# Gate and up of a feed-forward block by half-size products with features on partitions, and the residual stream parked in DRAM

## The chip, the core and the metric

The kernel runs on one core of one Trainium2 chip. The metric is the device time of one execution in microseconds; lower is better. Engines are named as the profile names them: PE (TensorE, with PEld for its weight loads), DVE (VectorE), ACT (ScalarE), POOL (GpSimd) and SP (SyncE, which issues nearly all DMAs).

## The reference

A trunk of two layers, each a SwiGLU half-step, a gated token mixing (stick-breaking, forgetting and memory attention) and a second SwiGLU half-step, with RMSNorm before and after each. There are 512 tokens of width 1024, all in float32. The change touches the four SwiGLU blocks only (D_FF = 2816 = 22 tiles of 128 features):

```python
def _swiglu(t, w_gate, w_up, w_down):
    return (jax.nn.silu(t @ w_gate) * (t @ w_up)) @ w_down

def reference(x, mem, ...):
    ...
    for l in range(DEPTH):
        f = _swiglu(_rmsnorm(h, ffn1_pre_g[l]), ffn1_w_gate[l], ffn1_w_up[l], ffn1_w_down[l])
        h = h + 0.5 * _rmsnorm(f, ffn1_post_g[l])
        u = _rmsnorm(h, mix_pre_g[l])
        ...
        h = h + _rmsnorm(merged @ w_out[l], mix_post_g[l])
        f = _swiglu(_rmsnorm(h, ffn2_pre_g[l]), ffn2_w_gate[l], ffn2_w_up[l], ffn2_w_down[l])
        h = h + 0.5 * _rmsnorm(f, ffn2_post_g[l])
    return h
```

## The kernel before

**Arithmetic.** Every float32 operand is split into a high part h (rounded for TensorE) and a low part l = x - h. A product is then three matmuls into one PSUM bank: h·h, h·l and l·h (`mm3`, L204; `split`, L177, makes the parts with a cast on ACT, L180, and a subtraction on DVE, L181). Weights come from DRAM in units of 512 KB (`Unit`): a load into a ring of two raw buffers, then a split into one of four `wh` and one of four `wl` buffers of 128 x 1024 elements. A weight buffer can be written again when the matmuls on the unit four earlier have read it.

**Order.** `Queue` holds the jobs of TensorE in the order in which they run; when a job starts, the units of the next jobs are split, four of them ahead (AHEAD, `load_ahead`), and loads are issued as far ahead as raw buffers are free (`fetch_ahead`). Between blocks, chains for the normalisation are woven in by estimated times (`weave`). Each engine executes its instructions in the order in which they stand in its queue, which is fixed when the kernel is built. DMAs stand in SP's queue, so a DMA whose buffer isn't free yet holds up those behind it.

**A feed-forward block** (`ffn`; "a0", "c0", "a1", "c1" in the names: tile `ga` is a gate weight of block a0 or a1, `uc` an up weight of c0 or c1). The normalised input stands transposed in `us`: model features on partitions, 512 tokens along the free dimension. Gate and up run by pairs of feature tiles (256 features): a 128x128 block of weights is stationary, 512 tokens move. The first pair runs in two token halves (`halved`), since the input arrives by token tiles; the other ten pairs in full width (`gates`, `ups`). `hidden` evaluates silu on ACT (L616) and the product with up on DVE.

**The down projection** of feature tiles 0 to 15 is already done by half-size products: in two sets ci = 0, 1 of eight tiles, the matrices are cut in 2 x 2 blocks and seven products of blocks take the place of eight (Winograd's form of Strassen's method). Number n = 0 to 6 names a product. The weight side is a `BlockUnit`: it loads a block, for n >= 2 subtracts blocks on DVE (L327, L335, L338), and is split. The other side, `first_factor`, adds and subtracts blocks of the hidden rows `hr` (L684 to L690) and is split as well. Three PSUM bank pairs hold partial sums (`SUM`: products 0, 3, 5 and 6 share one pair, 2 and 4 another); behind a product its sum is copied by ACT (L722) or added by DVE (L724) to the block `TO[n]` of the output. A product stays open in its bank while the next one of the same pair adds to it, so the next may not begin before the sum was read. In the queue one such product follows each gate or up job from pair 6/7 on, so that each is spread over two jobs. Tiles 16 to 21 go through plain matmuls in `down`, which also runs the end of the block with the next normalisation.

**The residual stream** `hT` is four tiles of 512 KB under the tag "o", which has eight buffers (`BUFS`, L102), from one normalisation to the next.

Of the kernel before, what the change touches and what calls it, by code (L numbers as in the profile page):

```python
# [9 lines left out]
F32 = mybir.dt.float32  # L10
# [7 lines left out]
P = 128  # L18
# [4 lines left out]
def kernel(  # L23
# [209 lines left out]
    class Unit:  # L233
# [11 lines left out]
        def ring(self):  # L245

            return self.place == "raw"

        def fetch(self):
            if not self.waits():  # L250
                return
            Q.fetched += self.ring()
# [27 lines left out]
    class BlockUnit(Unit):  # L280
# [15 lines left out]

        def ring(self):
            return self.BLOCKS[self.n] is not None
# [6 lines left out]
        def fetch(self):  # L305
# [3 lines left out]
            if self.n == 2:  # L309
                tc.keep_in_program_order(self.block(self.keep.get(0, self.k0), (0, 1)))  # L310
            if self.n == 3:
                tc.keep_in_program_order(self.block(self.keep.get(1, self.k0), (1, 1)))
            if self.ring():
                Q.fetched += 1
                self.raw = stile([P, self.nk, self.ncol], "raw", "raw_" + self.name, F32)
                self.block(self.raw[:], self.BLOCKS[self.n])

        def load(self):
# [3 lines left out]
            t = self.keep.get(0, self.k0) if self.n >= 2 else None  # L322
            b = self.keep.get(1, self.k0) if self.n >= 3 else None
            if self.n < 2:
                src = self.raw[:]
            elif self.n == 2:
                nc.vector.tensor_tensor(t, t, self.raw[:], ALU.subtract)  # L327
                src = t
            elif self.n == 3:
                nc.vector.tensor_tensor(t, b, t, ALU.subtract)  # L330
                src = t
            elif self.n == 4:
                src = b
            elif self.n == 5:
                nc.vector.tensor_tensor(b, b, self.raw[:], ALU.subtract)  # L335
                src = b
            else:
                nc.vector.tensor_tensor(t, t, self.raw[:], ALU.subtract)  # L338
                src = t
# [1135 lines left out]
```

## Time and profile before

| what | value |
|---|---|
| time, median of 3 runs | 2456.08 us (2452.51 to 2456.12) |
| span of the profiled execution | 2448.5 us |
| granted TensorE clock, mean | 0.999 |
| PE busy | 2432.6 us, 99% |
| DVE busy | 1550.9 us, 63% |
| ACT busy | 1181.7 us, 48% |
| data moved by DMA | 280.5 MB, 115 GB/s on the mean |

The span runs from the first to the last instruction of one profiled execution; the time of a run is measured on the device, without the profiler. A group of instructions is written as line, engine, operation, output<-inputs, shapes and count, then busy time in all and the mean of one in ns, then the idle time of the engine just before them and what ended it. In a timeline the first column is the start and the second the duration in us. Matmuls are pipelined: a matmul of 512 columns shows a duration of 0.39 us, but the next one starts sooner, so the pace is read from starts.

### The profile page before, as it was taken

Reading aid. Unit: us, or ns where it says so; the run is one execution under the profiler, and the core shown is the slowest. Engines: PE = TensorE matmul, PEld = TensorE weight load, DVE = VectorE, ACT = ScalarE, POOL = GpSimd, SP = SyncE. Lnnn points to the kernel's source line nnn. Section 1 sums busy time; section 2 is a strip of 40 time slices with the busy share of each in tenths; the row PEclk is TensorE's granted clock in tenths of the full one; section 3 lists DMA queues with packets and bytes.
Section 4 is the critical chain, followed back from the end, with each engine's and each line's share of the span. In section 5 each row is a group of like instructions: output and inputs, shape, how many; then the busy total and the mean of one; then the engine's idle time right before and its main releaser. Section 6 shows DMA issues by size and latency. Waiting matters only on the chain.

```text
span 2448.5 us, 31008 instructions
## 1 busy us (share of the span) xinstructions
PE 2432.6 (99%) x12167; PEld 2063.3 (84%) x12167; DVE 1550.9 (63%) x2220; ACT 1181.7 (48%) x1961; POOL 69.8 (3%) x124
## 2 busy tenths in 40 slices
PE   9999999999999999999999999999999999999998
PEld 8888889888888888888888888888888888888887
DVE  4364677678776653646644546866777866445466
ACT  4333365567655543333433333555776655333333
POOL 0000000000110000000000000000001100000000
PEclk9999999999999999999999999999999999999999
DMA  4334444222213433333424344442222243333433
GB/s 140 118 122 129 142 159 147 78 70 69 87 61 120 139 104 112 128 128 123 155 86 143 107 139 137 164 120 71 68 87 78 70 137 125 100 129 105 144 114 127
DMA packets 238598, 280.50 MB, mean 115 GB/s; under 512 B 8666, under 2 KB 188914, under 8 KB 238452
## 3 DMA queue, kind: packets, MB, share of 16 engines
q1 hardware_dynamic: 238356, 278.50, 35.5%
q8 instruction: 95, 1.56, 0.3%
q14 instruction: 51, 0.42, 0.0%
q0 software_dynamic: 96, 0.03, 0.0%
HBM read 272.20 MB, written 6.29 MB: 114 GB/s over the span
## 4 chain that ended last, share of the span: by engine, by line
PE 91%; DVE 4%; ACT 2%; DMA 1%; issue 1%; DVEq 0%; ACTq 0%
PE pg L207 3%; PE pg L206 3%; PE pg L208 3%; PE pgc L207 3%; PE puc L207 3%; PE pgc L208 3%; PE puc L208 3%; PE pgc L206 3%; PE puc L206 3%; PE pdc L207 3%; PE pdc L206 3%; PE pdc L208 3%; PE pga L206 3%; PE pga L208 3%; PE pua L208 3%; PE pga L207 3%
## 5 line engine op out<-in xcount | busy, mean ns | idle before, releaser
L206 PE MATMUL pg<-us_a,wh_wg 128*128 128x512 f32 x384 | 150.7, 392 | 0.0
L207 PE MATMUL pg<-us_a,wh_wg 128*128 128x512 f32 x384 | 149.8, 390 | 0.0
L208 PE MATMUL pg<-us_a,wl_wg 128*128 128x512 f32 x384 | 149.8, 390 | 0.0
L207 PE MATMUL pgc<-us_b,wh_gc 128*128 128x512 f32 x320 | 124.5, 389 | 0.0
L206 PE MATMUL pgc<-us_b,wh_gc 128*128 128x512 f32 x320 | 124.5, 389 | 0.0
L207 PE MATMUL puc<-us_b,wh_uc 128*128 128x512 f32 x320 | 124.5, 389 | 0.0
L208 PE MATMUL pgc<-us_b,wl_gc 128*128 128x512 f32 x320 | 124.5, 389 | 0.0
L208 PE MATMUL puc<-us_b,wl_uc 128*128 128x512 f32 x320 | 124.5, 389 | 0.0
L206 PE MATMUL puc<-us_b,wh_uc 128*128 128x512 f32 x320 | 124.5, 389 | 0.0
L181 DVE TENSOR_TENSOR wl_uc<-raw_uc,wh_uc 128x1024 fp32r<-128x1024 f32 x44 | 53.9, 1226 | 107.0 <-ACT wh_uc L180 107.0
L181 DVE TENSOR_TENSOR wl_ua<-raw_ua,wh_ua 128x1024 fp32r<-128x1024 f32 x44 | 53.8, 1225 | 98.4 <-ACT wh_ua L180 98.4
L180 ACT CAST wh_uc<-raw_uc 128x1024 fp32r<-128x1024 f32 x44 | 46.2, 1050 | 88.6 <-PE pgc L207 37.2
L181 DVE TENSOR_TENSOR wl_gc<-raw_gc,wh_gc 128x1024 fp32r<-128x1024 f32 x40 | 48.8, 1224 | 62.0 <-ACT wh_gc L180 61.7
L181 DVE TENSOR_TENSOR wl_ga<-raw_ga,wh_ga 128x1024 fp32r<-128x1024 f32 x40 | 48.8, 1224 | 61.0 <-ACT wh_ga L180 60.9
L208 PE MATMUL pda<-wh_da,ala 128*128 128x512 f32 x224 | 87.2, 389 | 0.0
L206 PE MATMUL pda<-wh_da,aha 128*128 128x512 f32 x224 | 87.2, 389 | 0.0
L208 PE MATMUL pdc<-wh_dc,alc 128*128 128x512 f32 x224 | 87.2, 389 | 0.0
L206 PE MATMUL pdc<-wh_dc,ahc 128*128 128x512 f32 x224 | 87.1, 389 | 0.0
L207 PE MATMUL pda<-wl_da,aha 128*128 128x512 f32 x224 | 87.1, 389 | 0.0
L207 PE MATMUL pdc<-wl_dc,ahc 128*128 128x512 f32 x224 | 87.1, 389 | 0.0
L208 PEld LDWEIGHTS pg<-us_a,wl_wg 128*128 128x128 f32 x384 | 72.2, 188 | 15.3
L180 ACT CAST wh_ua<-raw_ua 128x1024 fp32r<-128x1024 f32 x44 | 46.1, 1049 | 80.5 <-PE pga L207 34.1
(465 smaller groups left out, 7263.8 us busy)
## 6 DMA issues: line engine op xcount, KB each, us to landing
raw_da<-in_ffn_w_down_dram SPq DMA_DIRECT2D x58, 512.0 KB, 3.3
raw_dc<-in_ffn_w_down_dram SPq DMA_DIRECT2D x58, 512.0 KB, 3.3
raw_wg<-in_w_gate_dram SPq DMA_DIRECT2D x48, 512.0 KB, 3.5
raw_ga<-in_ffn_w_gate_dram SPq DMA_DIRECT2D x44, 512.0 KB, 3.6
raw_ua<-in_ffn_w_up_dram SPq DMA_DIRECT2D x44, 512.0 KB, 3.7
raw_gc<-in_ffn_w_gate_dram SPq DMA_DIRECT2D x44, 512.0 KB, 3.6
raw_uc<-in_ffn_w_up_dram SPq DMA_DIRECT2D x44, 512.0 KB, 3.7
raw_wo<-in_w_out_dram SPq DMA_DIRECT2D x24, 512.0 KB, 3.3
```

The source lines that it names most:

```text
L180: both = [nc.scalar.copy(h_ap, src)]
L181: make = lambda: nc.vector.tensor_tensor(l_ap, src, h_ap.bitcast(F32), ALU.subtract)
L206: nc.tensor.matmul(pt, lh, rh, start=start, stop=False, skip_group_check=free)
L207: nc.tensor.matmul(pt, lh, rl, start=False, stop=False, skip_group_check=free)
L208: nc.tensor.matmul(pt, ll, rh, start=False, stop=stop, skip_group_check=free)
```

## The change

Gate and up of tiles 0 to 15 are computed by seven half-size products too. A block's first (halved) pair is now tiles 16 and 17; then come gate and up of 18 and 19 in full width, during which `sums` builds the four token-side combinations u2 to u5 (eight additions on DVE, four splits). Then for each set of eight tiles seven gate products (`("G", ci)`) and seven up products (`("U", ci)`) follow. In each (`feature_product`) a 128x128 block of the weight combination is stationary, features come out on partitions, and a half of the tokens, 256 columns, moves. The order of the products is 0, 2, 1, 3, 4, 5, 6. Product 1 starts from a copy of product 0's sum (ACT copies between PSUM banks). Results: products 2 and 3 are copied by ACT, 4 and 5 are added by DVE, 1 and 6 go straight to silu (gate) or to the multiplication with silu (up); the blocks completed by 4 and 5 get theirs in one instruction of 1024 elements per partition.

After them the two sets of down products follow with the halves of gate and up of tiles 20 and 21 between some of them: the last five products of the second set stand together (`PLAN`). `("a", ci)` in it is the first factor of a set.

`BlockUnit` now loads one raw block in each of the seven products (eight loads with the kept tile, seven before) and has one kept tile instead of two; products 2, 3, 5 and 6 need one subtraction each. In gate and up one of a product's two units has its raw buffer in a second ring of two, under the tag "o" (`RINGS`). The kept tiles are there as well. The room comes from the residual stream: after the first pair `leave` writes its four tiles to DRAM (in the first block they are simply dropped, being x) and `back` reads them again ahead of the tail of `down`. The hidden rows keep their places.

The program has 2304 matmuls more than before, since in each block 768 of 512 columns become 1344 of 256. The core of the diff:

```diff
-        BLOCKS = ((0, 0), (1, 0), (0, 0), None, None, (0, 1), (1, 0))
-        def __init__(self, n, src, rows, k0, nk, ncol, keep, name):
+        BLOCKS = ((0, 0), (1, 0), (0, 0), (1, 1), (1, 1), (0, 0), (1, 0))
+        def __init__(self, n, src, rows, k0, nk, ncol, keep, name, place="raw"):
             super().__init__(src, k0, nk, 0, ncol, name)
-            self.n, self.rows, self.keep, self.fetched = n, rows, keep, False
+            self.n, self.rows, self.keep, self.fetched, self.place = n, rows, keep, False, place
         def waits(self):
...
             if self.n == 2:
-                tc.keep_in_program_order(self.block(self.keep.get(0, self.k0), (0, 1)))
-            if self.n == 3:
-                tc.keep_in_program_order(self.block(self.keep.get(1, self.k0), (1, 1)))
-            if self.ring():
-                Q.fetched += 1
-                self.raw = stile([P, self.nk, self.ncol], "raw", "raw_" + self.name, F32)
-                self.block(self.raw[:], self.BLOCKS[self.n])
+                tc.keep_in_program_order(self.block(self.keep.get(self.k0), (0, 1)))
+            Q.took(self.place, 1)
+            self.raw = stile([P, self.nk, self.ncol], self.place, "raw_" + self.name, F32)
+            self.block(self.raw[:], self.BLOCKS[self.n])
         def load(self):
             if self.h is not None:
                 return
             self.fetch()
-            t = self.keep.get(0, self.k0) if self.n >= 2 else None
-            b = self.keep.get(1, self.k0) if self.n >= 3 else None
-            if self.n < 2:
-                src = self.raw[:]
-            elif self.n == 2:
-                nc.vector.tensor_tensor(t, t, self.raw[:], ALU.subtract)
-                src = t
-            elif self.n == 3:
-                nc.vector.tensor_tensor(t, b, t, ALU.subtract)
-                src = t
-            elif self.n == 4:
-                src = b
-            elif self.n == 5:
-                nc.vector.tensor_tensor(b, b, self.raw[:], ALU.subtract)
-                src = b
-            else:
-                nc.vector.tensor_tensor(t, t, self.raw[:], ALU.subtract)
-                src = t
+            src = raw = self.raw[:]
+            if self.n in (2, 3, 5, 6):
+                t = self.keep.get(self.k0)
+                src = raw if self.n == 5 else t
+                a, b = (t, raw) if self.n in (2, 5) else (raw, t)
+                nc.vector.tensor_tensor(src, a, b, ALU.subtract)
             self.split_from(src)
-            if self.ring():
-                self.raw = None
-                Q.fetched -= 1
-            Q.fetch_ahead()
+            self.loaded()
...
+    RINGS = {"raw": BUFS["raw"], "o": 0}
...
+                        if un.place in RINGS and self.fetched[un.place] == RINGS[un.place]:
...
+    NG = 2
+    ORDER = (0, 2, 1, 3, 4, 5, 6)
+    SUM = (0, 1, 2, 0, 2, 0, 0)
+    TO = ((0, 0), (0, 0), (1, 1), (0, 1), (0, 1), (1, 1), (1, 0))
+    park = [nc.dram_tensor(f"park{i}", (NT, P, D), F32, kind="Internal").ap() for i in range(2 * L)]
+    def ffn(l, src, wg, wu, wd, dst, name, spare, parked, plan, aside=None):
...
+                leave()
+        def leave():
+            if parked is not None:
+                for t in range(NT):
+                    nc.sync.dma_start(parked[t], hT[t][:])
+            RINGS["o"] = 2
+            Q.fetch_ahead()
+        def back():
+            new_h(f"f{name}")
+            for t in range(NT):
+                if parked is not None:
+                    nc.sync.dma_start(hT[t][:], parked[t])
+                else:
+                    nc.sync.dma_start(hT[t][:], x[0, t * P:(t + 1) * P, :])
...
+        def sums():
+            whole = lambda nm: stile([P, 4, S // 2], "f", nm + name, F32)[:]
+            tt = nc.vector.tensor_tensor
+            def fp32(i, j):
+                t = whole(f"x{i}{j}")
+                tt(t, block(i, j, 0).bitcast(F32), block(i, j, 1).bitcast(F32), ALU.add)
+                return t
+            def pair(n, t):
+                h, l = (stile([P, 4, S // 2], "o" if n == 4 else "v", f"u{x}{name}_{n}")[:] for x in "hl")
+                split(h, l, t)
+                st["u", n] = h, l
+            x21 = fp32(1, 0)
+            s = fp32(1, 1)
+            yield
+            tt(s, x21, s, ALU.add)
+            pair(2, s)
+            yield
+            x11 = fp32(0, 0)
+            tt(s, s, x11, ALU.subtract)
+            pair(3, s)
+            yield
+            tt(x11, x11, x21, ALU.subtract)
+            tt(s, block(0, 1, 0).bitcast(F32), s, ALU.subtract)
+            tt(s, s, block(0, 1, 1).bitcast(F32), ALU.add)
+            yield
+            pair(4, s)
+            yield
+            pair(5, x11)
...
+        def in_product(n):
+            if n in (0, 1, 6):
+                i, j = ((0, 0), (0, 1), None, None, None, None, (1, 1))[n]
+                return [block(i, j, part) for part in range(2)]
+            return st["u", n]
+        def feature_product(ci, up, n, uns):
+            nm = f"{name}{'gu'[up]}_{ci}_{n}"
+            if n in (0, 1, 2):
+                st["c", n] = [pbank("z" if n == 0 else "mm", f"pw{nm}_{e}") for e in range(2)]
+            if n == 1:
+                for e in range(2):
+                    nc.scalar.copy(st["c", 1][e][:], st["c", 0][e][:])
+            if n == 0:
+                if not up:
+                    st["s", ci] = {}
+            pts = st["c", SUM[n]]
+            h, l = in_product(n)
+            opens, ends = n in (0, 2), n in (1, 4, 6)
+            for un in uns:
+                for k in range(un.nk):
+                    kk = un.k0 + k
+                    for f in range(FC // 2):
+                        c = slice(f * P, (f + 1) * P)
+                        o = pts[f // 2][:, (f % 2) * S // 2:(f % 2 + 1) * S // 2]
+                        mm3(o, un.h[:, k, c], un.l[:, k, c], h[:, kk], l[:, kk], opens and kk == 0 and f % 2 == 0,
+                            ends and kk == FC // 2 - 1, free=True)
+                        yield 3 * (S // 2) * PE_US
+            if n == 0:
+                return
+            q = TO[n]
+            g = st["s", ci]
+            if not up and q not in g:
+                g[q] = stile([P, FC // 2, S // 2], "f", f"s{name}_{ci}_{q[0]}{q[1]}", F32)[:]
+            g = g[q]
+            r = hidden_rows(2 * ci + q[1])[:, :, HALVES[q[0]]] if up else g
+            for e in range(2):
+                p = pts[e][:].rearrange("p (f q) -> p f q", f=2)
+                re, ge = r[:, 2 * e:2 * e + 2], g[:, 2 * e:2 * e + 2]
+                if n in (2, 3):
+                    nc.scalar.copy(re, p)
+                elif n in (4, 5):
+                    nc.vector.tensor_tensor(re, re, p, ALU.add)
+                elif up:
+                    nc.vector.tensor_tensor(re, p, ge, ALU.mult)
+                else:
+                    nc.scalar.activation(re, p, AF.Silu)
+            if n in (4, 5):
+                if up:
+                    nc.vector.tensor_tensor(r, r, g, ALU.mult)
+                else:
+                    nc.scalar.activation(r, r, AF.Silu)
+        def feature_products(ci, up):
+            w, nm = (wu if up else wg)[l, :, ci * FC * P:(ci + 1) * FC * P], f"{'gu'[up]}{name}_{ci}"
+            keep = Keep(lambda k0: stile([P, 2, S], "o", f"t{nm}_{k0}", F32)[:])
+            for n in ORDER:
+                uns = [BlockUnit(n, w, ND // 2, k, 2, S, keep, f"{nm}_{n}_{k}", ("raw", "o")[k // 2])
+                       for k in range(0, ND // 2, 2)]
+                yield uns, (lambda n=n, uns=uns: feature_product(ci, up, n, uns))
...
-            split(h, l, src, scale=-1.0 if n == 6 else None)
+            split(h, l, src)
...
+            keep = Keep(lambda k0: stile([P, 2, S], "o", f"bt{name}_{ci}_{k0}", F32)[:])
...
+    PLAN = [("g", 18), ("u", 18, "sums")] + 7 * [("G", 0)] + 7 * [("U", 0)] + 7 * [("G", 1)] + 6 * [("U", 1)] \
+        + [("a", 0), ("U", 1), ("d", 0), ("d", 0), ("g", 20, 0), ("d", 0), ("d", 0), ("g", 20, 1), ("d", 0), ("d", 0),
+           ("u", 20, 0), ("a", 1), ("d", 0), ("d", 1), ("d", 1), ("u", 20, 1)] + 6 * [("d", 1)]
```

More of the change, by code (lines that the diff above doesn't have):

```diff
@@ L372, in __init__ @@
             self.chains, self.t = [], 0.0
-            self.fetched = 0
+            self.fetched = {place: 0 for place in RINGS}
             self.pinned = False
@@ new lines, in beside @@
+        def beside(gen, steps, every):
+            for i, us_ in enumerate(gen):
+                if i % every == 0:
+                    next(steps, None)
+                yield us_
+            for _ in steps:
+                pass
+        def in_product(n):
[49 more added lines that the diff above has]
+                    nc.scalar.activation(r, r, AF.Silu)
@@ L768, in ffn @@
+        first_pair()
+        for what in plan:
+            queue(what)
+        for what in made.values():
+            assert isinstance(what, tuple) or not list(what)
+        if name == "a0":
+            Q.add([], vectors)
         if aside is not None:
             Q.add([], aside)
-        f0 = NC * FC
         hact = lambda k, c=FULL: (hid[f0 + k][:, 0, c], hid[f0 + k][:, 1, c])
-        down(wd[l, f0 * P:], NF - f0, hact, down_out, f"d{name}", dst, marks)
+        down(wd[l, f0 * P:], NF - f0, hact, down_out, f"d{name}", dst, marks, back)
```

111 lines of the change are left out of this document (55 added, 56 removed).

## The prediction

> **What bounds the kernel now.** I read the page first (busy shares, then the chain that ended last), after it the waits of TensorE, the stretches of the first feed-forward block, and single instructions in the order of time.
>
> ```profile
> span 2448.5 us, 31008 instructions
> PE 2432.6 (99%) x12167; PEld 2063.3 (84%) x12167; DVE 1550.9 (63%) x2220; ACT 1181.7 (48%) x1961; POOL 69.8 (3%) x124
> PE 91%; DVE 4%; ACT 2%; DMA 1%; issue 1%; DVEq 0%; ACTq 0%
> ```
> ```profile
> PE pts L944 <- ACT ts L973: 4.8, 2, 2.4
> PE warm L1345 <- DVE warm L1429: 1.2, 1, 1.2
> PE pgc L649 <- ACT us_b L183: 0.5, 2, 0.2
> ```
>
> TensorE is busy for 99% of the span, it is 91% of the chain, and its longest entry of waits is 4.8 us. So a matmul less is time saved, and a wait of TensorE that is new is time added in full. The vector engine's 63% is a mean; the stretches of block a0 tell more (columns: stretch, length, then busy us and instructions of PE, PEld, DVE, ACT, POOL; clock, DMA share, GB/s):
>
> ```profile
> 37.00:120.00 83.00, 83.00 (x372) 68.65 (x371) 30.62 (x29) 25.37 (x31) 1.08 (x2) 1.00 0.34 108
> 120.00:297.00 177.00, 177.00 (x782) 146.59 (x781) 104.38 (x102) 66.80 (x74) 0.00 (x0) 1.00 0.39 125
> 297.00:350.00 53.00, 52.62 (x240) 43.41 (x240) 37.52 (x57) 33.16 (x48) 0.00 (x0) 1.00 0.53 179
> 350.00:404.00 54.00, 53.84 (x338) 48.46 (x337) 44.11 (x72) 31.42 (x62) 0.00 (x0) 1.00 0.51 166
> ```
>
> DVE is at 37% where gate and up run alone, at 59% where half-size down products alternate with them, at 71 to 82% at the block's end. The alternation is what keeps DVE below TensorE: each down product's preparation is spread over its own matmuls and those of a gate or up job. The change uses that cover up.
>
> **What it removes on TensorE.** Per block 16 of the 22 feature tiles cost 16 x 2 x 8 x 3 = 768 matmuls of 512 columns. They become 28 products of 48 = 1344 matmuls of 256 columns. The pace of both widths, from the first and last row of a run of like matmuls (start, duration, engine, line; the second engine is the weight load):
>
> ```profile
> 99.95 0.39 PE L206 MATMUL pua<-us_x,wh_ua 128*128 128x512 f32 x1
> 101.99 0.39 PE L206 MATMUL pua<-us_x,wh_ua 128*128 128x512 f32 x1
> ```
> ```profile
> 28.44 0.28 PE L646 MATMUL pga<-us_x,w_ga 128*128 128x256 f32 x1
> 32.16 0.28 PE L647 MATMUL pga<-us_x,w_ga 128*128 128x256 f32 x1
> ```
> ```profile
> 28.33 0.19 PEld L646 LDWEIGHTS pga<-us_x,w_ga 128*128 128x128 f32 x1
> 30.37 0.19 PEld L647 LDWEIGHTS pga<-us_x,w_ga 128*128 128x128 f32 x1
> ```
>
> Nine steps in 2.04 us are 0.2267 us; 31 steps in 3.72 us are 0.120 us, with a weight load of 0.19 us behind each that starts every 0.120 us (17 steps in 2.04) and so hides. 768 x 0.2267 = 174.1 us, 1344 x 0.120 = 161.3 us: 12.8 us less per block, 51.3 us in four blocks. That is the whole possible gain; 256 columns give back 1344 x (0.120 - 0.1133) = 9 us of the eighth that seven products save.
>
> [...]
>
> **What it adds elsewhere.** Per block: 24 more weight splits (a cast on ACT, a subtraction on DVE), 32 more block subtractions on DVE, 8 additions and 4 splits for the sums of the token side, the copies, additions and products that gather the 28 results, and about 22 MB more loads, beside parking.
>
> ```profile
> L181 DVE TENSOR_TENSOR wl_uc<-raw_uc,wh_uc 128x1024 fp32r<-128x1024 f32 x44 | 53.9, 1226 | 107.0 <-ACT wh_uc L180 107.0
> L180 ACT CAST wh_uc<-raw_uc 128x1024 fp32r<-128x1024 f32 x44 | 46.2, 1050 | 88.6 <-PE pgc L207 37.2
> L327 DVE TENSOR_TENSOR bta<-bta,raw_da 128x1024 f32<-128x1024 f32 x8 | 9.8, 1224 | 3.4 <-DMA raw_da<-in_ffn_w_down_dram 3.4
> L724 DVE TENSOR_TENSOR fa<-fa,pda 128x512 f32<-128x512 f32 x40 | 26.6, 683 | 8.4 <-PE pda L208 8.4
> ```
> ```profile
> 316.87 1.28 DVE L724 TENSOR_TENSOR fa<-fa,pda 128x512 f32<-128x512 f32 x2
> 318.91 1.23 DVE L181 TENSOR_TENSOR wl_da<-bta,wh_da 128x1024 fp32r<-128x1024 f32 x1 [0.77 <-ACT wh_da L180]
> 320.05 1.22 DVE L338 TENSOR_TENSOR bta<-bta,raw_da 128x1024 f32<-128x1024 f32 x1
> 321.19 0.21 DVE L849 TENSOR_SCALAR mem_rstd<-mem_rstd 128x1 f32<-128x1 f32 x1
> ```
>
> Back to back, a 1024-column DVE instruction takes 1.14 us (318.91, 320.05, 321.19) and one of 512 columns 0.60 (two in 1.28, the last lasting 0.68); alone they show 1.22 and 0.68. A group of seven gate products has 14 splits, 8 subtractions and 4 additions of 512: 22 x 1.14 + 4 x 0.60 = 27.5 us; up adds two products of 1024 and four of 512, 32.2 us. TensorE needs 336 x 0.120 = 40.3 us. ACT has 14 casts and some ten 512-column operations, some 21 us. So on the average the new stage fits, and the sums are hidden behind the plain pair 18/19 (21.8 us of matmuls, 37% DVE before). DVE and ACT execute in the order built, however, so an average is not enough; three places don't fit.
>
> **Place one, between groups.** Products 5 and 6 of a group add into the same PSUM banks, one right behind the other: product 6 can't start before DVE has taken product 5's sum. In the built order DVE has ahead of those additions the first subtraction of the next group, on a tile whose load is issued only when product 6's first split has read it. From the start of product 4 on TensorE: its first half ends at 2.9 and frees the weight buffer (four buffers, a unit takes that of four units earlier); cast and split, 0.3 + 1.05 + 1.22, end at 5.6; the load is issued.
>
> ```profile
> raw_ga<-in_ffn_w_gate_dram SPq DMA_DIRECT2D x44, 512.0 KB, 3.6
> raw_da<-in_ffn_w_down_dram SPq DMA_DIRECT2D x58, 512.0 KB, 3.3
> bta<-in_ffn_w_down_dram SPq DMA_DIRECT2D x16, 512.0 KB, 4.7
> hsave<-hx SPq DMA_DIRECT2D x4, 512.0 KB, 2.8
> hm<-hsave SPq DMA_DIRECT2D x8, 512.0 KB, 6.5
> ```
>
> At 3.6 us it lands at 9.2. Behind it on DVE stand three instructions of 1.14 (that subtraction, product 6's second split, a split of the next group) and product 5's first addition: 13.3. TensorE had ended product 5 at 11.52 and has two matmuls (0.24 us) to fill: 1.55 us of waiting. Between up and gate a product of 1024 columns stands there too: 2.7. Three such places per block, 1.55 + 2.7 + 1.55 = 5.8, in four blocks 23 us. Bounds: nothing, if the load lands three microseconds sooner or DVE is ahead; 36 us at the 4.7 of the row whose tile is of the same kind. I take 3.6, since the stage's 16 loads in 40.3 us (208 GB/s) are not far above the 179 GB/s in which such loads still landed.
>
> **Place two, the second set of down products.** Before, a gate or up job stood between any two; now products 2 to 6 of the second set stand back to back. One needs 24 x 0.2267 = 5.44 us of TensorE. On DVE it has two splits, mostly two subtractions, one factor's sum and split, and two additions: 6 x 1.14 + 2 x 0.60 = 8.0. From the point where product 1's last split is done I count in the built order 27 instructions of 1024 and 12 of 512 up to product 5's additions, 38.0 us, and then product 6 must still run, about 5.3. TensorE has from there 1.7 of product 1, 5.44 of the last up job, five products (27.2) and eight matmuls of the tail (1.8): 36.1. It waits 38.0 + 5.3 - 36.1 = 7.2 us, in four blocks 29. Below: 0 only if DVE had a start of 7 us, for which the four weight buffers leave no room, so I put 5 per block; above: at the alone-standing 1.22 and 0.68, DVE needs 41.1 and the wait is 10.3, 41 us.
>
> **Place three, the first set.** Here up and gate halves stand between, yet product 2 waits for a subtraction that follows the new group's load, and product 6 for product 5's additions: by the same counting 0 to 3 us per block. I take 1.3, 5 us.
>
> **Parking.** Four stores of 512 KB per block (none in the first, which reads x again) and four loads. Stores landed in 2.8 us, loads in 6.5 when queued in fours; they are issued by SP behind the first pair and ahead of the tail, tens of microseconds before the residual is needed. SP's queue is held meanwhile: loads behind the second tile's load wait for product 6's split too, but each is wanted a product later. I put 2 us for all of it, 0 to 8. Cover gone, a late residual would cost one landing, 6.5 us per block.
>
> **Sum.** -51.3 + 23 + 29 + 5 + 2 = +8 us on a span of 2448.5: 2456. The median of the runs, 2456.08, lies 7.6 above the span, so runs of 2464.
>
> **Rivals.** *The group boundaries are hidden.* If the next group's tile lands earlier than DVE comes to it, only the down products wait: -51.3 + 29 + 5 + 2 = -15, **2441**. For it: DVE is free for a fifth to a third of that stage; loads of this size landed in 3.3 too. Against it: the load can't be issued sooner than the split, and the order on DVE is fixed.
>
> *DVE is the bound, and slower than at its best.* With DVE at 1.22 and 0.68 and landings of 4.7, which decide from about 4.2 us on: 36 + 41 + 8 + 5 - 51.3 = +39, **2495**. For it: 4.7 is the median landing of tiles of that kind before. Against it: 1.14 is seen wherever DVE works without a pause.
>
> *The weight load shows.* If a load of 0.19 us set the pace instead of hiding, 5376 x 0.07 = 376 us more, about 2840; against it stand the 31 steps at 0.120.
>
> *No waits at all*, the scheduler's order being kinder than I read it: **2405**.
>
> **How the numbers follow.** Chances: forecast 0.46, boundaries hidden 0.23, DVE slower 0.22, no waits 0.07, weight load 0.02. The forecast's own range is 2452 to 2479. The range 2437 to 2496 takes in both middle rivals and leaves out the last two and the far side of the third. A measurement of this kernel tells 0.2%, 4.9 us, from no change. Slower (over 2461): 0.22 + 0.02 + most of the forecast, 0.33 = 0.57. Within: 0.11 from the forecast and 0.02 from the first rival, 0.13. Faster: 0.07 + 0.21 + 0.02 = 0.30.
>
> **What would show it.** In the changed profile: 256-column steps of 0.120 us with 40.3 us for a group of seven; waits of TensorE for DVE's additions at three group boundaries per block, 1.5 to 2.7 us each, with DVE ahead of them idle for a DMA into the "t" tiles; in the second set of down products DVE at 95% or more and TensorE at about 80%, 7 us lost ahead of product 6 and its neighbours; DVE's total up by some 330 us; nothing waiting for parked tiles. I am wrong if boundary waits are gone or above 3 us, if DVE keeps up with the down products, or if TensorE loses time inside the groups, where I expect none.

## The result, and the profile after

| | time, median | profiled span |
|---|---|---|
| before | 2456.1 us (2452.5 to 2456.4) | 2448.5 us |
| after | 2490.0 us (2486.8 to 2492.1) | 2490.3 us |

The ratio is 1.0138, 95% interval 1.0126 to 1.015: slower by 34 us. The forecast was 2464, in a range of 2437 to 2496. The page of the changed kernel (busy time, share and instructions of each engine, then the shares of the chain that ended last, by engine and by line, then loads with the median from issue to landing):

```profile
span 2490.3 us, 36768 instructions
PE 2417.4 (97%) x14471; PEld 2139.7 (86%) x14471; DVE 1896.1 (76%) x2540; ACT 1338.0 (54%) x2147; POOL 70.9 (3%) x124
...
PE 67%; DVE 14%; DMA 12%; ACT 4%; issue 2%; DVEq 0%; ACTq 0%; SPq 0%
...
raw_da<-in_ffn_w_down_dram SPq DMA_DIRECT2D x74, 512.0 KB, 4.0
```

TensorE is 67% of the chain instead of 91%; DVE (14%, before 4%) and DMAs (12%, before 1%) have taken most of the rest. Stretches of block a0 in the changed kernel (columns as before the change: stretch, length, then busy us and instructions of PE, PEld, DVE, ACT, POOL; clock, DMA share, GB/s):

```profile
60.00:100.30 40.30, 40.30 (x335) 40.17 (x334) 29.69 (x29) 21.39 (x25) 0.00 (x0) 1.00 0.64 193
243.00:290.00 47.00, 43.82 (x190) 35.03 (x189) 38.26 (x35) 24.58 (x29) 0.00 (x0) 1.00 0.54 168
290.00:340.00 50.00, 43.78 (x172) 32.86 (x171) 44.21 (x53) 23.49 (x30) 0.00 (x0) 0.93 0.65 214
```

The first is inside the feature products: 335 matmuls in 40.3 us, TensorE never idle, ACT 21 us. The pace and the hidden weight loads are as forecast. The second is mostly the first set of down products, the third the second set: TensorE is idle for 3.2 and 6.2 us. The third shows also something not forecast, a granted clock of 0.93. In it DVE is busy for 88% and TensorE for 88%, where the prediction had 95% or more and 80%.

For a full account I worked out, from the starts of all matmuls in the trace, by how much each interval to the next matmul exceeds the step of its width (0.2267 us for 512 columns, 0.120 for 256), where the excess is over 0.04 us. Each excess is put down to the stage of the matmul that comes late, and summed over the four blocks. Intervals that begin with a matmul of another width are left out. The last column is all the rest: the begin, the plain pairs, the mixing stages and the transposes of the normalised rows.

```
excess, us          feature   down products          tail    rest   forecast
                    products  first set  second set
before                 -         0.1        0.0       0.5    22.1
changed kernel       14.4      18.0       36.4       10.6    35.3
forecast of change   23         5         29            2             -51.3 + 59
```

The excess rose by 92 us; 92 less the 51.3 that the matmuls became cheaper is 41, and the spans differ by 41.8. So the gain came in full, and the question is only where 92 us came from instead of 59. The medians differ by 34 and not by 42, because the table stands on one profiled execution of each kernel: nearly every run's time lies 1.8 us above its own span, so the profiled execution of before must have lain some 6 us under the median, and that of the changed kernel lay 2 above.

### The profile page after: what moved, and what is told of

It reads as the page before. It is cut to its first block, busy times and chain, and to the rows that moved or that the text cites. A ratio compares the mean times of both kernels' runs of the same rounds, so it can differ in the third digit from the quotient of the medians.

```text
span 2490.3 us, 36768 instructions
## 1 busy us (share of the span) xinstructions
PE 2417.4 (97%) x14471; PEld 2139.7 (86%) x14471; DVE 1896.1 (76%) x2540; ACT 1338.0 (54%) x2147; POOL 70.9 (3%) x124
## 4 chain that ended last, share of the span: by engine, by line
PE 67%; DVE 14%; DMA 12%; ACT 4%; issue 2%; DVEq 0%; ACTq 0%; SPq 0%
PE pg L206 3%; PE pg L207 3%; PE pg L208 3%; DMA raw_da<-in_ffn_w_down_dram 3%; DMA raw_dc<-in_ffn_w_down_dram 3%; DVE wl_da L181 2%; DVE wl_dc L181 2%; PE pb L208 2%; PE pb L206 2%; PE pb L207 2%; PE pwc0u L206 1%; PE pwc0u L208 1%; PE pwc0u L207 1%; PE pdc L207 1%; PE pwo L207 1%
## 5 line engine op out<-in xcount | busy, mean ns | idle before, releaser
L180 ACT CAST wh_dc<-raw_dc 128x1024 fp32r<-128x1024 f32 x50 | 52.6, 1052 | 74.9 <-PE pdc L208 28.0
L206 PEld LDWEIGHTS pg<-us_a,wh_wg 128*128 128x128 f32 x384 | 73.0, 190 | 14.6
L207 PEld LDWEIGHTS pg<-us_a,wh_wg 128*128 128x128 f32 x384 | 73.0, 190 | 14.5
L180 ACT CAST wh_da<-raw_da 128x1024 fp32r<-128x1024 f32 x50 | 52.5, 1051 | 60.4 <-DVE raw_da L316 17.6
L181 DVE TENSOR_TENSOR wl_dc<-raw_dc,wh_dc 128x1024 fp32r<-128x1024 f32 x50 | 61.0, 1222 | 29.8 <-ACT wh_dc L180 29.3
L184 DVE SCALAR_TENSOR_TENSOR wl_wg<-raw_wg,wh_wg 128x1024 fp32r<-128x1024 f32 x48 | 58.7, 1222 | 32.7 <-ACT wh_wg L183 32.4
L181 DVE TENSOR_TENSOR wl_da<-raw_da,wh_da 128x1024 fp32r<-128x1024 f32 x50 | 61.0, 1222 | 21.7 <-ACT wh_da L180 21.3
L183 ACT ACTIVATE wh_wg<-raw_wg 128x1024 fp32r<-128x1024 f32 x48 | 51.0, 1062 | 30.6 <-PE pv L1027 15.7
L180 ACT CAST wh_gc<-raw_gc 128x1024 fp32r<-128x1024 f32 x40 | 41.8, 1050 | 43.1 <-PE pwc0g L207 11.2
```

Source lines behind the costliest of these rows:

```text
L180: both = [nc.scalar.copy(h_ap, src)]
L181: make = lambda: nc.vector.tensor_tensor(l_ap, src, h_ap.bitcast(F32), ALU.subtract)
L183: both = [nc.scalar.activation(h_ap, src, AF.Copy, scale=scale)]
L184: make = lambda: nc.vector.scalar_tensor_tensor(l_ap, src, scale, h_ap.bitcast(F32), ALU.mult, ALU.subtract)
L206: nc.tensor.matmul(pt, lh, rh, start=start, stop=False, skip_group_check=free)
L207: nc.tensor.matmul(pt, lh, rl, start=False, stop=False, skip_group_check=free)
```

## The experiments

The excess by stage for every run that is told of below, with the median time and the ratio to the kernel before on the same chip (95% interval). The excess is that of the one profiled execution, which lay up to 6 us from the median (e4_both 2448.5, e7_fill 2487.4), so differences of a few us in a column mean little by themselves. Idle matmuls (e7, e10) are not counted as excess.

```
                feature  first set  second set  tail  rest    time     ratio
changed kernel   14.4      18.0       36.4      10.6  35.3   2490.0   1.0138 [1.0126, 1.0150]
e1_ring          16.3       3.1       35.6       0.9  29.4   2460.5   1.0021 [1.0005, 1.0036]
e2_order          6.0      19.9       34.6       4.7  28.7   2474.8   1.0079 [1.0064, 1.0094]
e3_nosub         12.9       1.1        7.7       9.6  25.9   2440.7   0.9942 [0.9927, 0.9957]
e4_both           5.9       2.1       35.7       0.9  27.5   2453.9   0.9993 [0.9983, 1.0004]
e5_pool           8.0      32.2       58.4       0.9  31.6   2507.9   1.0205 [1.0188, 1.0222]
e6_half           1.7       0.0        3.1       1.9  26.4   2442.7   0.9941 [0.9926, 0.9955]
e7_fill          16.7      21.6       32.1       1.3  30.0   2481.3   1.0103 [1.0085, 1.0120]
e8_spread         8.5       0.4       24.4       0.9  32.9   2439.2   0.9928 [0.9907, 0.9949]
e9_dorder         6.8       0.7        4.7       0.9  34.5   2424.6   0.9876 [0.9862, 0.9890]
e10_fill          7.2       0.4        8.4       0.9  34.6   2433.8   0.9912 [0.9898, 0.9925]
e11_nopark        7.2       0.8        3.8       0.9  29.9   2420.2   0.9861 [0.9845, 0.9878]
```

**e1_ring: four raw buffers in the down products.**

```diff
-                uns = [BlockUnit(n, w, FC // 2, k, 2, S, keep, f"d{name}_{ci}_{n}_{k}") for k in range(0, FC // 2, 2)]
+                uns = [BlockUnit(n, w, FC // 2, k, 2, S, keep, f"d{name}_{ci}_{n}_{k}", ("raw", "o")[k // 2])
+                       for k in range(0, FC // 2, 2)]
...
             if n == 0 and ci == 0:
-                RINGS["o"] = 0
                 dst.begin()
...
         def back():
+            RINGS["o"] = 0
             new_h(f"f{name}")
```

> The down products get the second ring of two raw buffers back (four in all). Theory A: the waits in the down products (54 us over four blocks in the changed kernel) are mostly the round trip of a raw buffer: two buffers, each held for a landing of 4.0 to 4.8 us, a cast and a split. Then they fall to the 30 us that DVE's instruction count alone gives, and the time to 2460 to 2468 us. Rival B: DVE's throughput alone sets them; then four buffers change nothing and the time stays at 2485 to 2490.

The reason to try it is the chain of waits of the changed kernel in block c0 (start, duration, what), where loads follow one another in a loop:

```profile
1128.67 1.06 ACT wh_dc L180
1129.76 1.24 DVE wl_dc L181
1131.02 4.56 DMA raw_dc<-in_ffn_w_down_dram
...
1139.27 4.77 DMA raw_uc<-in_ffn_w_up_dram
1144.13 1.06 ACT wh_uc L180
1145.22 1.24 DVE wl_uc L181
1146.47 4.34 DMA raw_dc<-in_ffn_w_down_dram
1150.83 1.23 DVE btc L316
1152.06 1.15 DVE wl_dc L181
1153.24 0.79 PE pdc L207
```

A raw buffer is split, the next load into it starts the moment the split ends, lands after 4.3 to 4.8 us, and is split at once: nothing is fetched ahead. With two more buffers the time fell by 30 us, to 2460.5, as theory A said. But not where it said: the second set of down products kept its waits (36.4 and 35.6), while the first set (18.0 to 3.1) and the tail (10.6 to 0.9) lost theirs, and the rest fell from 35.3 to 29.4.

**e2_order: no two neighbours in one PSUM bank.**

```diff
-    ORDER = (0, 2, 1, 3, 4, 5, 6)
+    ORDER = (0, 2, 3, 4, 5, 1, 6)
...
-            if n == 1:
+            if n == 2:
                 for e in range(2):
                     nc.scalar.copy(st["c", 1][e][:], st["c", 0][e][:])
```

> Order of the feature products 0, 2, 3, 4, 5, 1, 6 (product 1's start is copied beside product 2), so that no two neighbours share a PSUM bank. Theory: the 14 us of waits and half-speed matmuls at the group boundaries go down to about 3, time about 2479 us. Rival: the wait only moves into product 6's weights, since DVE still stands at the next group's subtraction; then over 2486.

2474.8 us, and the excess of the feature products fell from 14.4 to 6.0: the boundary is told rightly. It is not the whole gain of 15 us. The tail and the rest fell too, by 12.5 us in the profile, which the reason for the edit does not explain. What the boundary looks like in the changed kernel, in DVE's timeline at the end of block a0's first up group (in brackets the idle time before an instruction and what ended it):

```profile
129.24 1.32 DVE L762 TENSOR_TENSOR hra<-hra,pwa0u 128x512 f32<-128x512 f32 x2
132.77 1.23 DVE L316 TENSOR_TENSOR tga<-tga,raw_ga 128x1024 f32<-128x1024 f32 x1 [2.21 <-DMA tga<-in_ffn_w_gate_dram]
133.91 1.22 DVE L181 TENSOR_TENSOR wl_ua<-tua,wh_ua 128x1024 fp32r<-128x1024 f32 x1
135.05 1.22 DVE L769 TENSOR_TENSOR hra<-hra,sa 128x1024 f32<-128x1024 f32 x1
136.18 1.22 DVE L181 TENSOR_TENSOR wl_ga<-raw_ga,wh_ga 128x1024 fp32r<-128x1024 f32 x1
137.32 0.68 DVE L762 TENSOR_TENSOR hra<-hra,pwa0u 128x512 f32<-128x512 f32 x1
```

DVE adds product 4's sum at 129.24, has nothing to do but wait 2.2 us for the next group's tile, and then does four instructions before product 5's sum at 137.32. TensorE waits from 135.8 on.

**e3_nosub: without the down products' subtractions.**

```diff
-                nc.vector.tensor_tensor(src, a, b, ALU.subtract)
+                if self.name[0] != "d":
+                    nc.vector.tensor_tensor(src, a, b, ALU.subtract)
+                else:
+                    src = raw
```

> The weight-side block subtractions of the down products are left out (their raw blocks are split as loaded); all loads stay. DVE has 16 instructions of 1.14 us less per block, 73 us in all. Theory B (DVE's throughput): the waits of the down products vanish but for some 5 to 10 us, time about 2440. Theory A (two raw buffers): a pair of buffers still needs 4.4 + 1.05 + 1.22 = 6.7 us per product against 5.44 on TensorE, some 25 to 30 us of waits stay, time about 2462.

2440.7 us, with two raw buffers: theory B's number. The second set's waits fell from 36.4 to 7.7 and the first set's from 18.0 to 1.1, while the tail kept its 9.6. With e1_ring this divides the loss. The second set hangs on the subtractions, which more buffers don't help; whether by DVE's time or by the longer way from load to split, this run can't tell, and e9 will show that the number of instructions alone does not decide. The first set goes with either edit. The tail goes in every run with four buffers (0.9, in e6 1.9), but two buffers do not fix its size: it is 4.7 in e2 and 1.3 in e7.

**e4_both: both edits.**

> Four raw buffers in the down products and the order 0, 2, 3, 4, 5, 1, 6 together. If the two causes are separate, the gains add: about 24 + 11 us, time about 2455 us, no slower than before. If one feeds on the other (a backlog on DVE carried from the feature products into the down products), less than their sum.

2453.9 us: the gains of e1 and e2 are 29.5 and 15.2, and together 36.1, less than their sum of 44.7, since both take away waits of the tail. It is level with the kernel before (0.9983 to 1.0004). What is left is the second set.

**e5_pool: the down products' subtractions on POOL.**

```diff
+                eng = nc.gpsimd if self.name[0] == "d" else nc.vector
-                nc.vector.tensor_tensor(src, a, b, ALU.subtract)
+                eng.tensor_tensor(src, a, b, ALU.subtract)
```

> As e4_both, and the block subtractions of the down products' weights (16 per block) run on POOL instead of DVE. DVE theory: DVE is rid of 73 us in the one stage where it is behind; if POOL needs no more than 2.5 us for one, the remaining 38 us of waits in the down products fall to about 12 and the time to about 2430 us. Rival: POOL needs 4 us or more, or slows DVE down while it runs, and the time is 2454 us or more.

The rival, by the second of its two conditions: 2507.9 us. A group of the subtractions on POOL, then a group of DVE's splits in this run and the same group in e4_both (the mean of one in ns, then its idle time before them):

```profile
L317 POOL TENSOR_TENSOR btc<-raw_dc,btc 128x1024 f32<-128x1024 f32 x16 | 45.5, 2846 | 65.5 <-DMA raw_dc<-in_ffn_w_down_dram 42.0 <-DVE wl_dc L181 16.3 <-issue 7.2
...
L181 DVE TENSOR_TENSOR wl_dc<-raw_dc,wh_dc 128x1024 fp32r<-128x1024 f32 x50 | 72.3, 1446 | 31.8 <-ACT wh_dc L180 31.3
...
L181 DVE TENSOR_TENSOR wl_dc<-raw_dc,wh_dc 128x1024 fp32r<-128x1024 f32 x50 | 61.0, 1222 | 28.4 <-ACT wh_dc L180 28.2
```

One subtraction took 2.85 us instead of 1.22, and DVE was slowed down: its splits of 1024 elements that ran mostly beside a subtraction on POOL took 2.5 us on the mean, the others 1.26. So DVE, rid of 64 instructions, was busy for 1916.6 us against 1891.3 in e4. Besides, the load, ACT's cast and DVE's split wait for POOL in a row. The down products' excess rose from 37.8 to 90.6 us; how much of it is the longer chain and how much the slower DVE was not separated.

**e6_half: half of the change.** Tiles 8 to 15 go through plain pairs, with the first set's products between them, on top of e4.

```diff
-    PLAN = [("g", 18), ("u", 18, "sums")] + 7 * [("G", 0)] + 7 * [("U", 0)] + 7 * [("G", 1)] + 6 * [("U", 1)] \
...
+    PLAN = [("g", 18), ("u", 18, "sums")] + 7 * [("G", 0)] + 6 * [("U", 0)] + [("a", 0), ("U", 0)] \
+        + [("g", 8), ("d", 0), ("u", 8), ("d", 0), ("g", 10), ("d", 0), ("u", 10), ("d", 0), ("g", 12), ("d", 0),
+           ("u", 12), ("d", 0), ("g", 14), ("d", 0), ("a", 1), ("u", 14), ("d", 1), ("g", 20, 0), ("d", 1), ("g", 20, 1),
+           ("d", 1), ("d", 1), ("u", 20, 0), ("d", 1), ("d", 1), ("u", 20, 1), ("d", 1)]
```

> Half of the change: only tiles 0 to 7 by feature products, tiles 8 to 15 by plain pairs again, which stand between the first set's down products as before the change; with four raw buffers and the order 0, 2, 3, 4, 5, 1, 6. Half of the matmul gain is left, 25.7 us. Theory (what is lost is the cover of the down products): they wait no more than 2 us per block, the group boundary costs 1 us, time 2455 - 26 + 10 = about 2439 us. Rival (the losses lie in the feature products themselves, or in the end of a block): 2446 us or more.

2442.7 us, faster than before by 0.6%. The down products have 3.1 us of waits in all: covered by plain matmuls they cost what they did before the change.

**e7_fill: idle matmuls ahead of the second set's product 6 (a miss).**

```diff
+            if ci == 1 and n == 6:
+                spare = pbank("mm", f"fill{name}")
+                for _ in range(11):
+                    tc.keep_in_program_order(nc.tensor.matmul(spare[:], wsb[:, 0:P], wsb[:, 0:S], start=True, stop=True))
```

> The changed kernel with 11 idle bf16 matmuls of 512 columns ahead of product 6 of each block's second set, where TensorE waits 3.0 to 3.5 us; they write a bank that nobody reads. Theory (a wait of over about 2 us is followed by some 4 us of matmuls at half speed): the matmuls behind the wait run at 0.227 us instead of 0.427, about 2 us per block, time about 2482 us. Rival (the slow matmuls have another cause, such as the loads under way): they stay slow and the time stays at 2490 or rises.

The theory's numbers are from the changed kernel: in block a0 TensorE waits 2.87 us until 324.22, and behind it the steps from 327.71 to 330.27 are 0.427 us. The time fell as far as the theory said, to 2481.3, but not by its way: the long wait (2.78 us in block a0) stands ahead of product 5, not 6, so that the idle matmuls came behind it, and the half-speed matmuls stayed (ten steps of 0.427 us from 324.22 on). The tail's excess fell from 10.6 to 1.3: TensorE comes to the tail later by the idle work, and finds its weights split. That is no gain, since the 44 idle matmuls take 0.216 us each, 9.5 us in all. The profiled span is 4.6 us shorter than the changed kernel's; why the median fell by 9 stays open. e10 puts the idle matmuls right.

**e8_spread: the last pair's halves spread evenly** over the 14 down products, on top of e4.

```diff
-        + [("a", 0), ("U", 1), ("d", 0), ("d", 0), ("g", 20, 0), ("d", 0), ("d", 0), ("g", 20, 1), ("d", 0), ("d", 0),
-           ("u", 20, 0), ("a", 1), ("d", 0), ("d", 1), ("d", 1), ("u", 20, 1)] + 6 * [("d", 1)]
+        + [("a", 0), ("U", 1), ("d", 0), ("d", 0), ("d", 0), ("g", 20, 0), ("d", 0), ("d", 0), ("g", 20, 1), ("d", 0),
+           ("a", 1), ("d", 0), ("d", 1), ("d", 1), ("u", 20, 0), ("d", 1), ("d", 1), ("u", 20, 1), ("d", 1), ("d", 1),
+           ("d", 1)]
```

> As e4_both, with the four halves of gate and up of tiles 20 and 21 spread evenly over the 14 down products, instead of three in the first set and one in the second. DVE theory with a total: DVE needs 8.0 us per product against 5.44 on TensorE in both sets, so spreading only lets each half cover one product's excess; the second set's 38 us of waits fall by 5 to 10, time 2444 to 2449 us. Rival: the first set now waits for what the second gains, time 2452 to 2456 us.

2439.2 us, better than the best end of what was expected. The second set's excess fell from 35.7 to 24.4, and the first set's didn't rise (2.1 to 0.4). Of the 24.4, 22.8 stand at product 5. TensorE there (duration 0.39 us for a matmul of 512 columns at full speed):

```profile
312.53 0.39 PE L208 MATMUL pda<-wh_da,ala 128*128 128x512 f32 x1
315.00 0.50 PE L206 MATMUL pda<-wh_da,aha 128*128 128x512 f32 x1 [2.08 <-ACT aha L180]
...
317.07 1.22 PE L208 MATMUL pda<-wh_da,ala 128*128 128x512 f32 x2 [0.81 <-DVE ala L181]
318.09 0.63 PE L206 MATMUL pda<-wh_da,aha 128*128 128x512 f32 x1
...
322.36 0.60 PE L207 MATMUL pda<-wl_da,aha 128*128 128x512 f32 x1
322.79 0.41 PE L208 MATMUL pda<-wh_da,ala 128*128 128x512 f32 x1
323.03 0.39 PE L206 MATMUL pda<-wh_da,aha 128*128 128x512 f32 x1
```

It waits 2.1 us for product 5's first factor, then 0.8 for its low part, and then comes a run of ten steps in 4.27 us (318.09 to 322.36), 0.427 us each instead of 0.2267.

**e9_dorder: the down products in the order 0, 2, 3, 4, 5, 1, 6 too,** on top of e8.

```diff
-                first_factor(ci, n + 1)
+                first_factor(ci, ORDER[ORDER.index(n) + 1])
...
-            for n in range(7):
+            for n in ORDER:
```

> As e8_spread, and the down products too in the order 0, 2, 3, 4, 5, 1, 6, so that the products whose first factor and weights need least of DVE (1 and 6) stand at the end, apart from product 5. Theory: in each block the 2.24 us wait ahead of the second set's product 5 and the half-speed matmuls behind it (5 us per block in all) shrink to 1 or 2 us, time 2422 to 2430 us. Rival: the backlog is DVE's total, not its order; the wait moves to another product, time 2436 to 2440 us.

2424.6 us, within the theory's numbers, and 1.24% faster than before: the best version of those that leave no work out. Its page, and two stretches of block a0 (the second holds most of the second set):

```profile
span 2422.6 us, 36664 instructions
PE 2393.3 (99%) x14471; PEld 2133.6 (88%) x14471; DVE 1889.1 (78%) x2540; ACT 1337.6 (55%) x2147; POOL 70.7 (3%) x124
```
```profile
243.00:290.00 47.00, 47.00 (x208) 38.70 (x207) 40.97 (x41) 20.52 (x23) 0.00 (x0) 1.00 0.60 200
290.00:325.00 35.00, 33.20 (x145) 26.25 (x143) 30.79 (x39) 20.77 (x28) 0.00 (x0) 1.00 0.56 194
```

DVE has the same work as in the changed kernel (1889 and 1896 us) and TensorE is back at 99%: with four buffers and the halves spread, the loss was not DVE's total, but what stands ahead of what.

**e10_fill: idle matmuls inside the wait,** e8 with the edit of e7 at product 5 and 8 matmuls.

> As e8_spread, with 8 idle bf16 matmuls (1.8 us) ahead of product 5 of each block's second set, inside the wait of 2.24 us that TensorE has there; they write a bank that nobody reads. Theory (a wait of 2 us costs a second time, by some 12 matmuls at 0.43 us instead of 0.227): with the wait filled they run at 0.227, product 5 starts no later, and the time falls by 4 x 2.3 us to about 2430. Rival (the slow matmuls come from something else): they stay, time 2439 or more.

TensorE at the same place (the bf16 row is the idle ones, of which the trace has seven of eight):

```profile
312.82 1.67 PE L824 MATMUL filla<-warm 128*128 128x512 bf16 x7
314.83 0.50 PE L206 MATMUL pda<-wh_da,aha 128*128 128x512 f32 x1 [0.34 <-ACT aha L180]
...
316.91 0.73 PE L208 MATMUL pda<-wh_da,ala 128*128 128x512 f32 x2 [0.88 <-DVE ala L181]
317.48 0.40 PE L206 MATMUL pda<-wh_da,aha 128*128 128x512 f32 x1
317.71 0.40 PE L207 MATMUL pda<-wl_da,aha 128*128 128x512 f32 x1
```

Product 5 starts no sooner (its factor is as late as before), but its matmuls now run at 0.23 us a step (17 steps in 3.89 us from 317.48 on). The second set's excess fell from 24.4 to 8.4; some 7 us of this fall is only the wait, now filled with idle work. The time fell by 5.4 us where 9 were expected, and the intervals of the two ratios overlap. The pace is the better evidence: 0.427 us a step in e8 and 0.23 at the same place in e10, with a mean granted clock of 0.993 and 0.996 in the two profiled executions. That this wait of TensorE was followed by slow matmuls, and that none followed once work without any use filled most of it, is shown for block a0.

**e11_nopark: without storing the residual,** on top of e9.

```diff
-                 park[2 * l] if l else None, PLAN, lambda l=l, mn=mn: mem_norm(l, mn))
+                 None, PLAN, lambda l=l, mn=mn: mem_norm(l, mn))
...
-        mc = ffn(l, subs[i + 2], ffn2_w_gate, ffn2_w_up, ffn2_w_down, subs[i + 3], f"c{l}", "o", park[2 * l + 1], PLAN)
+        mc = ffn(l, subs[i + 2], ffn2_w_gate, ffn2_w_up, ffn2_w_down, subs[i + 3], f"c{l}", "o", None, PLAN)
```

> As e9_dorder, but the residual stream is not stored in any block: the tail of every block reads x in its place (so the residual that is added is x's; the four stores of 512 KB in three blocks are left out, the loads stay). Theory: the stores are hidden behind the first pair and cost nothing, time 2424 us within 5. Rival: they hold up SP's queue or the loads of the first feature products, time 2415 us or less.

2420.2 us, ratio 0.9861 (0.9845 to 0.9878) against 0.9876 (0.9862 to 0.9890): the stores cost 4 us or nothing, the intervals overlap. In the changed kernel no entry of TensorE's waits names a parked tile.

## Why the prediction was right in sign and short in size

Slower was forecast, and slower it is, but by 34 us and not by 8. That 2490 lies within 2437 to 2496 is luck: that range had been drawn to take in the rival at 2495, whose mechanism did not occur, and the forecast's own range ended at 2479.

- **The matmuls** (-51.3 us): right. 335 in 40.3 us within the feature products, and the account closes to within 1 us of the two spans. DVE's total rose by 345 us, near the 330 foretold. The loads did not rise by 22 MB a block beside parking: DMAs moved 371.1 MB instead of 280.5, and without the 28 transfers of 512 KB that parking needs that is 19 MB a block; no term of the sum rests on it.
- **Between groups** (23 us): right in mechanism, too high. DVE idles for the "t" tile as foretold, but the excess is 14.4 us, some 11 of it waits. Between up and gate in block a0 the two waits cost 2.3 us in place of 2.7; ahead of the first up group the tile landed as DVE came to it (0.9 us of idle time, 0.1 us for TensorE), in place of 1.55.
- **The second set of down products** (29 us): right in size, in part by luck. 36.4 us, of which some 26 are waits and 10 half-speed matmuls that were not foreseen. e3 shows that it hangs on the subtractions, e1 that it is not the buffers. But the wait stands mostly ahead of product 5 (21.9 us), for its first factor, and not ahead of 6, and DVE was not full: 88% in block a0 where 95% was foretold. e9 has the same instructions in another order and a spread plan, and an excess of 4.7.
- **The first set** (5 us, bound 12): mis-sized, 18.0 us. The step was "by the same counting": I counted DVE instructions for it, but the two raw buffers decide. They make TensorE wait for round trips of a load of 4 to 4.8 us, a cast and a split; e1 takes 15 of the 18 away (e3 17, since without the subtraction a buffer is free sooner). The ring of two stands nowhere in the prediction's count for the down products.
- **"2 us for all of it, 0 to 8"** (parking and what else hangs on SP's queue): this is the step that failed most, since no other term of the sum stands for the tail and the rest. The tail cost 10.1 us and the rest 13.2 more than before. The stores had little part in it (e11: 0 to 4 us); the loads back were left out in no run, but no wait of TensorE names a parked tile. The tail's waits are for weight splits, and with four buffers its excess is gone, so it is the raw ring again: there two buffers leave little fetched ahead.
- **The rest** stays open. The ring does not explain it: it is 25.9 in e3 with two buffers and 34.5 in e9 with four, against 22.1 before. Much of the rise stands right behind the blocks, where transposes wait, mostly for DVE: 6.0 us in the changed kernel and 7.4 in e9, 0.2 before. What holds DVE up there was not tested.
- **Half speed** had no term. The granted clock was 0.992 on the mean instead of 0.999, which over 2490 us is up to 17 of the 92 us; it is spread over all columns.
- **From span to time** the forecast added 7.6 us. In nearly every run it is 1.8; the other 5.8 must have been the profiled execution's distance from the median.

The rival "DVE is the bound, and slower than at its best" gave 2495, near the time, but is not what happened. DVE kept its step of 1.14 us (129.24 to 137.32 above), and its place was taken by the ring and by TensorE's slow matmuls. Landings of the "t" tiles did go up to about 5 us (that rival used 4.7), as the DMA view of the changed kernel shows (size, median us from issue to landing), and those of the raw blocks to 3.9 to 4.5 from 3.3 to 3.7, which lengthens the ring's round trip:

```profile
tga<-in_ffn_w_gate_dram SPq DMA_DIRECT2D x8, 512.0 KB, 5.1
tua<-in_ffn_w_up_dram SPq DMA_DIRECT2D x8, 512.0 KB, 5.0
```

## What to carry to other kernels

Trading matmuls for vector work pays by what stands beside the new work, not by an engine's mean: here the same matmuls and vector instructions gave 2490 us and 2425, depending on order and on two load buffers. Count for each ring of load buffers the round trip (landing, cast, split: in block c0 above 4.3 to 4.8, 1.06 and 1.24 us) against the time of the work that one filling feeds; a ring that sufficed while something else stood between stops sufficing when that is taken away. And look for what an engine meets in its built order ahead of the one instruction that the bottleneck waits for (under e2, a wait of 2.2 us and four instructions of 1.14). Work moved to an idle engine slowed the busy one down in e5, where a subtraction took 2.85 us on POOL and the group of DVE's splits shown there 1446 ns on the mean instead of 1222: look at the time of one instruction on both.

## What the runs showed of the hardware that I had not expected

Waits of TensorE cost a second time here. In the changed kernel, behind the 1.6 us wait at 137.45 and one of 0.2 at 138.05, matmuls of 256 columns run at 0.12 us until 139.2 and then at 0.21 us:

```profile
137.45 0.38 PE L208 MATMUL pwa0g<-us_x,wl_ga 128*128 128x256 f32 x1 [1.62 <-DVE wl_ga L181]
138.05 0.39 PE L206 MATMUL pwa0u<-us_x,wh_ua 128*128 128x256 f32 x1 [0.21 <-DVE hra L762]
...
139.37 0.41 PE L207 MATMUL pwa0u<-us_x,wh_ua 128*128 128x256 f32 x1
139.58 0.41 PE L208 MATMUL pwa0u<-us_x,wl_ua 128*128 128x256 f32 x1
...
142.57 0.36 PE L207 MATMUL pwa0u<-us_x,wh_ua 128*128 128x256 f32 x1
142.76 0.28 PE L208 MATMUL pwa0u<-us_x,wl_ua 128*128 128x256 f32 x1
```

The slow stretch begins over a microsecond after the wait has ended and lasts from 139.3 to 142.7. The granted clock (third number from the end) is 0.50 in it and 1.00 ahead of it. The other two stretches below are from block c1, where waits of 1.6 and 0.2 us were followed by no slow matmuls:

```profile
135.90:139.30 3.40, 1.63 (x11) 1.44 (x12) 3.37 (x5) 0.66 (x1) 0.00 (x0) 1.00 0.92 290
139.32:142.73 3.41, 3.41 (x18) 3.41 (x17) 2.80 (x3) 0.30 (x1) 0.00 (x0) 0.50 0.61 166
...
2245.30:2248.70 3.40, 1.82 (x14) 1.47 (x12) 3.40 (x4) 1.04 (x1) 0.00 (x0) 1.00 0.79 230
2248.70:2252.10 3.40, 3.18 (x27) 3.14 (x27) 3.37 (x5) 0.03 (x1) 0.00 (x0) 1.00 0.75 238
```

The clock records of the changed kernel's trace hold ten stretches at 0.50 that end within the execution. Nine are 3.41 us long and one, from 323.6 in block a0, 6.83, and they start whole multiples of 3.413 us from one another. I added up TensorE's idle time in pieces of 3.41 us, counted from these starts, from 10 us on. The piece ahead of each of the ten has 1.77 to 2.86 us of it: 1.77 in the one from 135.9, 2.29 in the one from 320.2. The piece from 2245.3 has 1.58, since the second wait fell into the next, and of all the pieces with no slow stretch behind them the most is 1.71 (from 388.5). So in this trace the idle time of such a piece tells the two places apart, where the lengths of the waits do not. In the kernel before, a piece counted likewise from its one such stretch (from 606.0) has 1.95 us, most of a wait of 2.37, and no slow matmuls behind it; what decides was not shown.

In e8 the matmul at 315.80, ahead of the wait of 0.8 us, lasts 0.47 us already (in e10 the one at 315.64 lasts 0.39), so the slow stretch begins there, behind the wait of 2.1 alone. In e10, with 1.67 us of idle matmuls in that wait, the steps are 0.23 us.
